# An order written out for the first feed-forward product, with sums begun early and a last product left in PSUM

## The chip, the cores and the metric

The kernel runs on one core of a Trainium2 chip. The core has TensorE (PE) for matmuls, VectorE (DVE), ScalarE (ACT), GpSimd (POOL) and SyncE (SP). Each works through its own list of instructions in order, and semaphores tie the lists together. SP and POOL issue DMA transfers here, and in one place of the changed kernel ACT does. The metric is the time of one execution on the device, in microseconds. The profiled execution is a separate one; its trace is what the times of single instructions are read from.

## The reference

A trunk of two layers over 512 positions of width 1024, in float32. Each layer has an attention part (two kinds of heads) and a feed-forward part; a last norm follows. What matters here is the feed-forward part:

```python
h = rmsnorm(x, mlp_norm[l])
u = jnp.square(jax.nn.relu(jnp.einsum('bsd,df->bsf', h, w_ff1[l])))   # 1024 -> 4096
x = x + jnp.einsum('bsf,fd->bsd', u, w_ff2[l])                        # 4096 -> 1024
...
return rmsnorm(x, final_norm)
```

## The kernel before

**Arithmetic.** A float32 matmul is made of three in a reduced type: each operand is split into a high part and a low rest, and `three` (L281 to L285) adds hi x hi (L283), hi x lo and lo x hi (L284, L285; lines named by the operands in the profile). Every weight tile of 128x1024 must so be split before TensorE uses it: ACT rounds it into `whi` (L125), then DVE takes the difference `wlo` (L126). Weight units are numbered through the kernel. A unit's split is written a few units ahead of its matmuls (`W.next`, `do_split`), into a small ring of pairs of buffers, so that a split waits until an earlier pair is used up.

**The feed-forward part** goes in four groups of the hidden width for each layer, eight in all: L0 g0 to g3, L1 g0 to g3. In a group both products are done by a Strassen-like scheme with seven instead of eight part products:

- The first product has seven "q" products, in the order `HALVES` = 1, 2, 5, 6, 7, 3, 4, each in two halves c = 0, 1 of 24 matmuls of 128x256. Their results add up in PSUM banks: products 1, 6, 7 and 4 share bank a (names f10.. with c), 2 has its own, 5 and 3 share b.
- Between them stand the taps (`tap`): product 1 is copied to F1 by ACT (L907); 2 is added by DVE (L909) and bent, that is relu and square by ACT (L903, L904, `bend`); 6 is copied to F0 (L912); 7 is copied to F2 (L914), has b added (L915) and is bent; 3 is added to F0 (L920) and bent; 4 is bent into F3 straight from PSUM. Since 7 adds onto the same bank as 6, its matmuls wait for the copy of 6.
- The second product has seven forms, `FORMS` = 11, 21, x1, 22, x2, x3, x4, each in two halves of 12 matmuls of 128x512. Their left operand is a table F that is split too (`roll`, L231): Ah and Al, for the x forms Ahx and Alx. DVE adds their results to Y (L948).

**Weights that are sums.** The raw weights of products 7, 5, 6 and 3 are sums of quarters of the weight matrix. Quarters named 11, 12, 21, 22 are loaded by SP (`fill`, L783); a second quarter is added by an accumulating DMA issued by POOL, or a tile is added by DVE (`sum1`, L795):

- tile y: 11 = weight of product 1; later y + 21 = weight of 7 (POOL, L797);
- tile z: 12 = weight of product 2;
- tile x: 21 + 22 = weight of 5 (POOL, L785); then x + y = weight of 6 (DVE); then that + z = weight of 3 (DVE);
- tile w: 22 = weight of 4.

Each tile exists for both halves c (names q00/q01 for x, yw00/yw01 or q10/q11 for y, q20/q21 for z, ww and cs for w). `then(kind, g, form, c, fn, ...)` hangs a function behind the split of that unit. The weights of the forms are fetched by SP (L802) and for the sum forms added by POOL (L809).

**What sets the order.** Within an engine a scheduler places what the program writes, by dependencies and its own estimate. `line(a, v)` overrides it: every operation given to it is chained behind the one given before on ACT or on DVE. Before, the splits of units "f" and "q", the rolls of the forms, the results of forms and some of the tail go through `line`; taps and sums don't.

**The tail.** In the last group `gather` adds x4's results onto Y (L948), `square` sums the squares of a row of tiles (L983), `root` adds the parts (L988) and POOL raises them to -1/2 (L990), `weigh` multiplies by the final gains (L994), and `store` scales and stores (L1000, L1002, DMA on SP).

Of the kernel before, what the change touches and what calls it, by code (L numbers as in the profile page):

```python
# [48 lines left out]
HALVES = ("1", "2", "5", "6", "7", "3", "4")  # L49
FSLOT = {"11": 1, "21": 3, "x1": 4, "22": 3, "x2": 1, "x3": 0, "x4": 2}  # L50
# [112 lines left out]
def trunk(ctx, tc, xT, w, w1, w2, gains, gfin, lamv, cos, sin, out):  # L163
    nc = tc.nc
# [154 lines left out]
    for l in range(L):  # L319
        last = l == L - 1  # L320
        with ExitStack() as actx:
# [470 lines left out]
            def sum1(what, g, c):  # L792
                i = _AT[("q", l, g, "5", c)]
                t, by = W.raw[i], W.raw[_AT[("q", l, g, "1" if what == "y" else "2", c)]]
                nc.vector.tensor_add(t, t, by)  # L795
                if what == "y":
                    nc.gpsimd.dma_start(by, quad1(g, "21", c), accum_op=ALU.add)  # L797
# [50 lines left out]
            for g in range(GROUPS):  # L848
                for c in range(GP // 2):
                    then("q", g, "5", c, sum1, "y", g, c)  # L850
                    then("q", g, "6", c, sum1, "z", g, c)
                    then("q", g, "2" if g else "7", c, fetch, g, "21", c)
                    then("q", g, "7", c, fetch, g, "22", c)
                    then("q", g, "3", c, fetch, g, "11", c)
                    if g:
                        then("q", g, "5", c, fill, "w", g, c)
# [7 lines left out]
                    if g + 1 < GROUPS:  # L864
                        then("q", g, "7", c, fill, "y", g + 1, c)
# [11 lines left out]
        with ExitStack() as fctx:  # L877
# [20 lines left out]
            def tap(q, c, pt):  # L898
# [3 lines left out]
                def bend(n, scale=1.0, src=None):  # L902
                    nc.scalar.activation(f(n), f(n) if src is None else src, AF.Relu, scale=scale)  # L903
                    nc.scalar.activation(f(n), f(n), AF.Square)  # L904

                if q == "1":
                    nc.scalar.copy(f(1), pt)  # L907
                elif q == "2":
                    nc.vector.tensor_add(f(1), f(1), pt)  # L909
                    bend(1)  # L910
                elif q == "6":
                    nc.scalar.copy(f(0), pt)  # L912
                elif q == "7":
                    nc.scalar.copy(f(2), pt)  # L914
                    nc.vector.tensor_add(f(2), f(2), sums[("b", c)])  # L915
                    bend(2, -1.0)
                elif q == "4":
                    bend(3, -1.0, pt)
                elif q == "3":
                    nc.vector.tensor_add(f(0), f(0), pt)  # L920
                    bend(0)
# [10 lines left out]
            def less(o, i, j):  # L932
                nc.vector.scalar_tensor_tensor(
                    out=F[o], in0=F[i], scalar=-1.0, in1=F[j], op0=ALU.mult, op1=ALU.subtract)
# [28 lines left out]
            def lay(tb, j):  # L963
                o = place(tb, j)
                n = 24 * j + tb
                nc.vector.scalar_tensor_tensor(
                    out=o, in0=turned(tb, j), scalar=fin[:, n : n + 1], in1=o, op0=ALU.mult, op1=ALU.add)
# [228 lines left out]
```

## Time and profile before

| | us |
|---|---|
| median of three runs | 1145.57 |
| lowest and highest run | 1143.81, 1146.23 |
| the profiled execution's own time | 1145.74 |
| its span in the profile | 1144.0 |
| TensorE busy | 1118.7 |
| VectorE, ScalarE, GpSimd busy | 923.9, 707.9, 173.5 |
| DMA moved | 183.39 MB |

The span is what the engines and queues of the core cover in the trace; 1.74 us of the execution lie around it. A row of the trace in order of time has start and duration in us, the engine, the line, the operation, output <- input, and in brackets the idle time of that engine ahead of it with what ended it. A row of the waits has who waited <- for whom: us in total, times, longest. A group's matmuls on product 7 appear as `f<-T_hi,whi`, since all the products share L283.

### The profile page before, as it was taken

What the parts mean: (1) busy time and instruction counts of PE and PEld (TensorE: products, weight loads), DVE (VectorE), ACT (ScalarE), POOL (GpSimd) and SP (SyncE); (2) the same over time, 40 slices, a digit from 0 to 9 for tenths busy, and PEclk for the clock granted to TensorE, in tenths of its full rate; (3) what the DMA queues carried; (4) which work ended last, traced back from release to release, by engine and by line L of the source; (5) the groups of instructions that cost most, each with busy time, mean ns of one, the idle gap of its engine ahead of it and who ended that gap; (6) DMA issues with size and microseconds to landing.
All of it is one profiled execution on the core that took longest, in us unless ns stands there. A gap on an engine that the chain in (4) does not pass through costs nothing. (4 is left out here: it accounts for less than half of the span.)

```text
span 1144.0 us, 18030 instructions
## 1 busy us (share of the span) xinstructions
PE 1118.7 (98%) x6834; PEld 996.7 (87%) x6834; DVE 923.9 (81%) x1238; ACT 707.9 (62%) x1121; POOL 173.5 (15%) x253
## 2 busy tenths in 40 slices
PE   9999999999998999999999999999999999999996
PEld 7889889899898898899878898888998998988985
DVE  6898778898886877877879876887978788788786
ACT  6456666677747547557545566665777575565674
POOL 1001432110110110201000024231101102011012
PEclk9999999999999999999999999999999999999998
DMA  7664443255886776886526844423568858859764
GB/s 254 178 177 138 127 132 111 101 133 170 189 200 179 153 189 181 186 212 171 113 74 184 204 115 125 147 93 127 114 198 173 219 148 187 219 119 206 209 133 125
DMA packets 60470, 183.39 MB, mean 160 GB/s; under 512 B 7520, under 2 KB 8544, under 8 KB 60384
## 3 DMA queue, kind: packets, MB, share of 16 engines
q1 hardware_dynamic: 46416, 131.88, 35.9%
q0 software_dynamic: 13824, 50.34, 25.1%
q8 instruction: 54, 0.88, 0.3%
q14 instruction: 32, 0.26, 0.1%
q10 hardware_dynamic: 144, 0.02, 0.0%
HBM read 154.95 MB, written 2.10 MB: 137 GB/s over the span
## 5 line engine op out<-in xcount | busy, mean ns | idle before, releaser
L126 DVE TENSOR_TENSOR wlo<-q,whi 128x1024 fp32r<-128x1024 f32 x184 | 223.1, 1220 | 29.4 <-ACT whi L125 28.9
L125 ACT ACTIVATE whi<-q 128x1024 fp32r<-128x1024 f32 x184 | 189.2, 1050 | 68.6 <-DMA q<-in_w 31.6
L283 PE MATMUL f<-T_hi,whi 128*128 128x256 f32 x512 | 146.6, 286 | 7.7 <-ACT F L912 7.6
L284 PE MATMUL f<-T_lo,whi 128*128 128x256 f32 x512 | 145.6, 284 | 0.0
L285 PE MATMUL f<-T_hi,wlo 128*128 128x256 f32 x512 | 145.5, 284 | 0.0
L809 POOL DMA_DIRECT2D q<-in_w x64 | 56.2, 912 | 367.9 <-DVE wlo L126 348.2
L283 PE MATMUL f<-h_hi,whi 128*128 128x256 f32 x384 | 109.8, 286 | 1.0 <-DVE F L915 0.9
L284 PE MATMUL f<-h_lo,whi 128*128 128x256 f32 x384 | 108.6, 283 | 0.0
L285 PE MATMUL f<-h_hi,wlo 128*128 128x256 f32 x384 | 108.6, 283 | 0.0
L283 PEld LDWEIGHTS f<-T_hi,whi 128*128 128x128 f32 x512 | 98.9, 193 | 9.2 <-ACT F L912 9.2
L285 PEld LDWEIGHTS f<-T_hi,wlo 128*128 128x128 f32 x512 | 99.0, 193 | 0.0
L284 PEld LDWEIGHTS f<-T_lo,whi 128*128 128x128 f32 x512 | 98.9, 193 | 0.0
L126 DVE TENSOR_TENSOR wlo<-raw,whi 128x1024 fp32r<-128x1024 f32 (+1 forms) x68 | 79.2, 1172 | 7.6 <-ACT whi L125 7.5
L125 ACT ACTIVATE whi<-raw 128x1024 fp32r<-128x1024 f32 (+1 forms) x68 | 66.3, 982 | 29.4 <-PE p1d1q L284 6.4
L283 PEld LDWEIGHTS f<-h_hi,whi 128*128 128x128 f32 x384 | 73.5, 192 | 2.5 <-DVE F L915 1.6
L284 PEld LDWEIGHTS f<-h_lo,whi 128*128 128x128 f32 x384 | 73.6, 192 | 0.3
L285 PEld LDWEIGHTS f<-h_hi,wlo 128*128 128x128 f32 x384 | 73.6, 192 | 0.1
L231 ACT ACTIVATE Ahx<-F 128x1024 fp32r<-128x1024 f32 x32 | 33.9, 1061 | 53.6 <-PE x L284 23.7
L231 DVE TENSOR_TENSOR Alx<-F,Ahx 128x1024 fp32r<-128x1024 f32 x32 | 39.2, 1226 | 9.4 <-ACT Ahx L231 9.4
L126 DVE TENSOR_TENSOR wlo<-yw,whi 128x1024 fp32r<-128x1024 f32 x24 | 29.3, 1222 | 15.5 <-ACT whi L125 15.5
L125 ACT ACTIVATE whi<-yw 128x1024 fp32r<-128x1024 f32 x24 | 25.3, 1054 | 26.3 <-DMA yw<-in_w 24.7
L904 ACT ACTIVATE F<-F 128x512 f32<-128x512 f32 x64 | 40.2, 630 | 1.5
(950 smaller groups left out, 3316.7 us busy)
## 6 DMA issues: line engine op xcount, KB each, us to landing
q<-in_w SPq DMA_DIRECT2D x100, 512.0 KB, 4.7
q<-in_w POOLq DMA_DIRECT2D x84, 512.0 KB, 6.4
raw<-in_w SPq DMA_DIRECT2D x62, 512.0 KB, 4.0
yw<-in_w SPq DMA_DIRECT2D x12, 512.0 KB, 4.8
yw<-in_w POOLq DMA_DIRECT2D x12, 512.0 KB, 7.9
cs<-in_w SPq DMA_DIRECT2D x8, 512.0 KB, 4.6
ww<-in_w SPq DMA_DIRECT2D x8, 512.0 KB, 4.7
x<-in_xT SPq DMA_DIRECT2D x8, 256.0 KB, 4.5
```

Of the source, the lines that this page charges most:

```text
L125: h = nc.scalar.activation(hi[:, a:b], raw[:, a:b], AF.Copy)
L126: self.last = h, nc.vector.tensor_tensor(out=lo[:, a:b], in0=raw[:, a:b], in1=hi[:, a:b].bitcast(F32), op=ALU.subtract)
L231: return nc.scalar.activation(hi, src, AF.Copy), nc.vector.tensor_tensor(out=lo, in0=src, in1=hi.bitcast(F32), op=ALU.subtract)
L283: nc.tensor.matmul(pt, ah, bh, start=first, stop=False, skip_group_check=onto)
L284: nc.tensor.matmul(pt, ah, bl, start=False, stop=False, skip_group_check=onto)
L285: nc.tensor.matmul(pt, al, bh, start=False, stop=last, skip_group_check=onto)
L809: paced(nc.gpsimd.dma_start(t, quad(g, q, c), accum_op=ALU.add))
L904: nc.scalar.activation(f(n), f(n), AF.Square)
```

## The change

The names of the functions stay, the line numbers shift (in the changed kernel whi is L126, wlo L127, product 1's copy L912, product 2's add L914, bends L908 and L909, product 6's copy L917, product 7's copy and add L919 and L920, product 3's add L925, the rolls L232, results of forms L953).

1. The accumulation of 21 onto y is issued behind the split of product 1 (`grow_y`). The weight of 6 is then the new y plus w (`sum_y`), behind 5's second split for c = 0 and behind 6's first for c = 1; the weight of 3 is that plus z (`sum_z`). The load of w moves to the form stage of the group before, and that of form 21's weights from product 2 to 5.
2. All taps, bends, sums, rolls and differences of the feed-forward part go through `line`, so ACT and DVE keep the order in which the program writes them: the split that is due, then the product's tap.
3. In the last group x4's PSUM banks take x3's sum with Y added in place, squares and stores read PSUM, part of the adding for the norm moves to POOL, and the very last store is issued by ACT.
4. The places at which x is laid into Y in layer 1's middle groups are given by a table `LAYS`.

```diff
+LAYS = (("5", 1), ("6", 0), ("6", 1), ("7", 0))
...
-            def sum1(what, g, c):
-                i = _AT[("q", l, g, "5", c)]
-                t, by = W.raw[i], W.raw[_AT[("q", l, g, "1" if what == "y" else "2", c)]]
-                nc.vector.tensor_add(t, t, by)
-                if what == "y":
-                    nc.gpsimd.dma_start(by, quad1(g, "21", c), accum_op=ALU.add)
+            def grow_y(g, c):
+                nc.gpsimd.dma_start(W.raw[_AT[("q", l, g, "7", c)]], quad1(g, "21", c), accum_op=ALU.add)
+
+            def sum_y(g, c):
+                t, by, w = (W.raw[_AT[("q", l, g, q, c)]] for q in "674")
+                line(v=nc.vector.tensor_add(t, by, w))
+
+            def sum_z(g, c):
+                t, by = (W.raw[_AT[("q", l, g, q, c)]] for q in "32")
+                line(v=nc.vector.tensor_add(t, t, by))
...
-                    then("q", g, "5", c, sum1, "y", g, c)
-                    then("q", g, "6", c, sum1, "z", g, c)
-                    then("q", g, "2" if g else "7", c, fetch, g, "21", c)
+                    then("q", g, "1", c, grow_y, g, c)
+                    then("q", g, "56"[c], 1 - c, sum_y, g, c)
+                    then("q", g, "6", c, sum_z, g, c)
+                    then("q", g, "5" if g else "7", c, fetch, g, "21", c)
...
-                    if g:
-                        then("q", g, "5", c, fill, "w", g, c)
...
                     if g + 1 < GROUPS:
+                        then("f", g, "11", c, fill, "w", g + 1, c)
...
                 def bend(n, scale=1.0, src=None):
-                    nc.scalar.activation(f(n), f(n) if src is None else src, AF.Relu, scale=scale)
-                    nc.scalar.activation(f(n), f(n), AF.Square)
+                    line(nc.scalar.activation(f(n), f(n) if src is None else src, AF.Relu, scale=scale))
+                    line(nc.scalar.activation(f(n), f(n), AF.Square))
...
                 elif q == "6":
-                    nc.scalar.copy(f(0), pt)
+                    line(nc.scalar.copy(f(0), pt))
...
+            def finish_row(tb, pt):
+                if tb == 0:
+                    store(2, 0)
+                    store(2, 1)
+                square(tb, 0, pt)
+                root(tb, 0)
+                if tb == 0:
+                    store(3, 0)
+                    store(3, 1)
+                    store(0, 0, pt)
+                else:
+                    store(0, 1)
+                    store(1, 0, pt)
+                    store(1, 1, None, nc.scalar)
...
+                        elif tail and form == "x3":
+                            line(v=nc.vector.tensor_add(to[r], to[r], place(r, 0)))
...
```

How this moves instructions, in the group L0 g2 (whi92 to whi101 are the splits of 5 c0, 5 c1, 6 c0, 6 c1, 7 c0, 7 c1, 3 c0, 3 c1, 4 c0, 4 c1; F10 is product 2's table, F00 that of 6 and 3, F20 that of 7).

ACT, from the split of 5 c1 to the first copy of product 6, before:

```order
L125 ACTIVATE whi93_4409<-q01_0_2671 128x1024
L907 COPY F10_2679<-f1020_4383 128x512
L907 COPY F10_2679<-f1021_4416 128x512
L125 ACTIVATE whi94_4442<-q00_0_2670 128x1024
L125 ACTIVATE whi95_4475<-q01_0_2671 128x1024
L903 ACTIVATE F10_2679<-F10_2679 128x512
L904 ACTIVATE F10_2679<-F10_2679 128x512
L125 ACTIVATE whi96_4512<-yw00_2870 128x1024
L903 ACTIVATE F10_2679<-F10_2679 128x512
L904 ACTIVATE F10_2679<-F10_2679 128x512
L231 ACTIVATE Ah110_4508<-F10_2679 128x1024
```

and in the changed kernel:

```order
L126 ACTIVATE whi93_4409<-q01_0_2671 128x1024
L912 COPY F10_2679<-f1021_4415 128x512
L126 ACTIVATE whi94_4441<-q00_0_2670 128x1024
L908 ACTIVATE F10_2679<-F10_2679 128x512
L909 ACTIVATE F10_2679<-F10_2679 128x512
L126 ACTIVATE whi95_4475<-q01_0_2671 128x1024
L908 ACTIVATE F10_2679<-F10_2679 128x512
L909 ACTIVATE F10_2679<-F10_2679 128x512
L232 ACTIVATE Ah110_4508<-F10_2679 128x1024
L126 ACTIVATE whi96_4512<-yw00_2872 128x1024
```

The bends of product 2 have moved ahead of the splits whi95 and whi96; three splits and then the copy of product 6 follow in both.

DVE over the same stretch, before:

```order
L126 TENSOR_TENSOR wlo93_4410<-q01_0_2671,whi93_4409 128x1024
L795 TENSOR_TENSOR q00_0_2670<-q00_0_2670,yw00_2870 128x1024
L795 TENSOR_TENSOR q01_0_2671<-q01_0_2671,yw01_2871 128x1024
L126 TENSOR_TENSOR wlo94_4443<-q00_0_2670,whi94_4442 128x1024
L909 TENSOR_TENSOR F10_2679<-F10_2679,f2020_4447 128x512
L795 TENSOR_TENSOR q00_0_2670<-q00_0_2670,q20_0_2674 128x1024
L126 TENSOR_TENSOR wlo95_4476<-q01_0_2671,whi95_4475 128x1024
```

and in the changed kernel:

```order
L127 TENSOR_TENSOR wlo93_4410<-q01_0_2671,whi93_4409 128x1024
L798 TENSOR_TENSOR q00_0_2670<-yw00_2872,ww0_2874 128x1024
L127 TENSOR_TENSOR wlo94_4442<-q00_0_2670,whi94_4441 128x1024
L802 TENSOR_TENSOR q00_0_2670<-q00_0_2670,q20_0_2674 128x1024
L798 TENSOR_TENSOR q01_0_2671<-yw01_2873,cs_76 128x1024
L914 TENSOR_TENSOR F10_2679<-F10_2679,f2020_4447 128x512
L127 TENSOR_TENSOR wlo95_4476<-q01_0_2671,whi95_4475 128x1024
```

Two sums now stand between wlo94 and the add of product 2, and the second y sum has moved behind wlo94.

POOL, around weight 5 of the group, before:

```order
L809 DMA q01_0_2671<-in_w2 128x1024
L785 DMA q00_0_2670<-in_w1 128x1024
L785 DMA q01_0_2671<-in_w1 128x1024
L797 DMA yw00_2870<-in_w1 128x1024
L797 DMA yw01_2871<-in_w1 128x1024
```

and in the changed kernel:

```order
L814 DMA q01_0_2671<-in_w2 128x1024
L786 DMA q00_0_2670<-in_w1 128x1024
L794 DMA yw00_2872<-in_w1 128x1024
L786 DMA q01_0_2671<-in_w1 128x1024
L794 DMA yw01_2873<-in_w1 128x1024
```

The first accumulation onto y has moved between the two of weight 5. Further on, ACT has the bends of 7 between the splits of 4 and of form 11; from the split of 4 c0 on, in the changed kernel (before, whi101 and whi102 stood ahead of the first bend):

```order
L126 ACTIVATE whi100_4634<-ww0_2874 128x1024
L919 COPY F20_2680<-f1020_4383 128x512
L908 ACTIVATE F20_2680<-F20_2680 128x512
L909 ACTIVATE F20_2680<-F20_2680 128x512
L126 ACTIVATE whi101_4666<-cs_76 128x1024
L919 COPY F20_2680<-f1021_4415 128x512
L908 ACTIVATE F20_2680<-F20_2680 128x512
L909 ACTIVATE F20_2680<-F20_2680 128x512
L126 ACTIVATE whi102_4698<-q00_0_2670 128x1024
```

Each split now stands behind the bends of the half before it. TensorE at the start of form 21, in the changed kernel (before, each pair of Ah matmuls was followed by its Al, and the matmul of x1 stood in its own form):

```order
L286 MATMUL 11021_4835<-whi103_4731,Al110_4509 128x512
L284 MATMUL 21020_4862<-whi104_4767,Ah210_4829 128x512
L285 MATMUL 21020_4862<-wlo104_4768,Ah210_4829 128x512
L284 MATMUL 21021_4863<-whi104_4767,Ah210_4829 128x512
L285 MATMUL 21021_4863<-wlo104_4768,Ah210_4829 128x512
L284 MATMUL x1020_4906<-whi106_4880,Ahx10_4876 128x512
L286 MATMUL 21020_4862<-whi104_4767,Al210_4830 128x512
```

The first matmul with Al210 has moved behind one of x1, which needs the table Ahx10 and the split whi106.

More of the change, by code (lines that the diff above doesn't have):

```diff
@@ L919, in tap @@
                 elif q == "3":
[L920 removed]
+                    line(v=nc.vector.tensor_add(f(0), f(0), pt))
                     bend(0)
@@ L1051, in trunk @@
                                 less(3, 1, 3)
-                            if last and g in (1, 2) and q in "5673":
-                                lay("5673".index(q), g - 1)
                 chains = {}
@@ L1073, in trunk @@
                         W.do_split(W.used + 1 + r, first)
[L1074 to L1084 removed]
+                        tail = end and last
                         if end and not last and form in ("21", "x2", "x3", "x4"):
                             line(v=add_to(tb, j, to[r]))
+                        elif tail and form == "x4":
+                            finish_row(r, to[r])
                         else:
```

74 lines of the change are left out of this document (34 added, 40 removed).

## Prediction

> **What bounds the kernel now.** I read the busy times first, then the chain of waits by engine, then the places that it names in order of time. Line numbers are those of the kernel before. First, TensorE's busy line and waits:
>
> ```profile
> PE 1118.7 (98%) x6834; PEld 996.7 (87%) x6834; DVE 923.9 (81%) x1238; ACT 707.9 (62%) x1121; POOL 173.5 (15%) x253
> PE f L283 <- ACT F L912: 7.6, 6, 3.1
> PE f L283 <- DVE F L915: 0.9, 2, 0.5
> ACT whi L125 <- DMA yw<-in_w: 24.7, 8, 5.2
> ```
>
> TensorE has little left to give. What the change can win in the feed-forward part is 7.6 + 0.9 us: product 7 waits for the copy that empties its PSUM bank of product 6 (L912), and product 3 for L915. What it can lose is larger, since TensorE is the bound nearly everywhere: any list of ACT and DVE that ends after its product is due comes out at the end. So I follow one group, layer 0's third, on both engines from the moment when weight 5's second half is there. ACT, then DVE:
>
> ```profile
> 413.31 1.06 ACT L125 ACTIVATE whi<-q 128x1024 fp32r<-128x1024 f32 x1 [2.06 <-DMA q<-in_w]
> 419.81 0.64 ACT L903 ACTIVATE F<-F 128x512 f32<-128x512 f32 x1 [0.73 <-DVE F L909]
> 420.47 0.63 ACT L904 ACTIVATE F<-F 128x512 f32<-128x512 f32 x1
> 424.78 1.06 ACT L125 ACTIVATE whi<-yw 128x1024 fp32r<-128x1024 f32 x1 [3.67 <-DMA yw<-in_w]
> 428.97 1.99 ACT L125 ACTIVATE whi<-q 128x1024 fp32r<-128x1024 f32 x2
> 430.86 0.56 ACT L912 COPY F<-f 128x512 f32<-128x512 f32 x1
> 414.40 1.22 DVE L126 TENSOR_TENSOR wlo<-q,whi 128x1024 fp32r<-128x1024 f32 x1 [1.90 <-ACT whi L125]
> 415.55 2.35 DVE L795 TENSOR_TENSOR q<-q,yw 128x1024 f32<-128x1024 f32 x2
> 417.95 1.23 DVE L126 TENSOR_TENSOR wlo<-q,whi 128x1024 fp32r<-128x1024 f32 x1
> 419.09 0.68 DVE L909 TENSOR_TENSOR F<-F,f 128x512 f32<-128x512 f32 x1
> ```
>
> The start of the list is the landing of weight 5 (413.31), and its end is L912 at 430.86. In between ACT stands idle 3.67 us for weight 7, which the late accumulating transfer brings. These rows give the steps for the sums below: whi to its wlo 1.09; a DVE operation over 1024 columns to the next 1.14 (two take 2.35); L909 0.68; relu to square 0.65 and square to the next 0.53; whi after whi 0.96 (two take 1.99); L912 0.56.
>
> **First part: the list from weight 5 to product 7.** The new order on ACT is: 5's last split, 6 first half, the two bends of product 2 first half, 6 second half, its bends, Ah of form 11, the two splits of 7, 3's first, then the copy of product 6. DVE has two sums for each half between the splits and the adds. From the start S of the split of 5's second half: its wlo 1.09, first y sum to 3.45, whi of 6 at 3.55, wlo at 4.64, z sum 5.78, the second half's y sum 6.92, L909 8.06 to 8.74, relu 8.77, square 9.42, whi of 6's second half only then, 9.95, wlo 11.04, z sum 12.18, L909 13.32, bends 14.03 and 14.68, Ah 15.35, whi 16.31, 17.27 and 18.23, copy L912 19.19 to 19.75, product 7 at S + 19.80. Weight 7 is there early now, so the 3.67 us are gone, but nothing of them is left: the extra z and y sums and the bends ahead of 6's second half have taken their place. The six groups with this order, S first and then product 7's first matmul as it was:
>
> ```profile
> 330.33 1.06 ACT L125 ACTIVATE whi<-q 128x1024 fp32r<-128x1024 f32 x1 [1.38 <-DVE fin L1032]
> 493.82 1.06 ACT L125 ACTIVATE whi<-q 128x1024 fp32r<-128x1024 f32 x1 [0.82 <-DMA q<-in_w]
> 899.86 1.06 ACT L125 ACTIVATE whi<-q 128x1024 fp32r<-128x1024 f32 x1 [2.12 <-DMA q<-in_w]
> 979.13 1.06 ACT L125 ACTIVATE whi<-q 128x1024 fp32r<-128x1024 f32 x1 [2.11 <-DMA q<-in_w]
> 1060.05 1.06 ACT L125 ACTIVATE whi<-q 128x1024 fp32r<-128x1024 f32 x1 [1.41 <-DMA q<-in_w]
> 349.84 0.39 PE L283 MATMUL f<-T_hi,whi 128*128 128x256 f32 x1 [3.10 <-ACT F L912]
> 431.48 0.39 PE L283 MATMUL f<-T_hi,whi 128*128 128x256 f32 x1 [1.34 <-ACT F L912]
> 511.94 0.39 PE L283 MATMUL f<-T_hi,whi 128*128 128x256 f32 x1 [1.47 <-ACT F L912]
> 917.11 0.38 PE L283 MATMUL f<-T_hi,whi 128*128 128x256 f32 x1 [0.99 <-ACT F L912]
> 997.66 0.38 PE L283 MATMUL f<-T_hi,whi 128*128 128x256 f32 x1 [0.15 <-ACT F L912]
> 1077.99 0.38 PE L283 MATMUL f<-T_hi,whi 128*128 128x256 f32 x1
> ```
>
> S + 19.80 less the start before: 0.29, 1.63, 1.68, 2.55, 1.27, 1.86, together **+9.3 us** with weight 5 landing where it does now.
>
> **Where weight 5 lands.** On POOL the early accumulation of y's first half now stands between the two halves of 5 in the same queue.
>
> ```profile
> 403.54 0.88 POOL L785 DMA_DIRECT2D q<-in_w  x1 [11.89 <-DMA q<-in_w]
> 406.11 0.88 POOL L785 DMA_DIRECT2D q<-in_w  x1 [1.70 <-DMA q<-in_w]
> 341.59 1.06 ACT L125 ACTIVATE whi<-yw 128x1024 fp32r<-128x1024 f32 x1 [5.20 <-DMA yw<-in_w]
> 344.09 1.06 ACT L125 ACTIVATE whi<-yw 128x1024 fp32r<-128x1024 f32 x1 [0.25 <-DMA yw<-in_w]
> ```
>
> Its issue alone costs nothing: 0.88 us fit into the 1.70 us that POOL waits for the plain load of the second half. Its bytes don't: two accumulations issued back to back were taken up 2.50 us apart (341.59 and 344.09, both waiting for the transfer), so 5's second half comes 0 to 3 us later. Against that, the loads of w and form 21 leave this stretch. I take half, 1.4 us, six times: **+8.4 us** (bounds 0 and 18). The Trainium skill, page "DMA: Bandwidth & Descriptors", section "Anatomy of one DMA — SWDGE (gpsimd) path", puts the part of a transfer that grows with its size at bytes / 436e9 s, an estimate of 1.2 us for 512 KB. By that the term would be 7.2 us; the trace's 2.50 us say that sharing makes it more.
>
> **The two first groups of the layers** have opening operations in the same lists. There weight 5 is early, and the pace is DVE's:
>
> ```profile
> 817.10 1.22 DVE L826 TENSOR_TENSOR hx1mdl<-hx1mdl 128x1024 f32<-128x1024 f32 x1
> 834.35 0.28 PE L283 MATMUL f<-T_hi,whi 128*128 128x256 f32 x1
> 266.12 0.39 PE L283 MATMUL f<-T_hi,whi 128*128 128x256 f32 x1 [0.56 <-ACT F L912]
> ```
>
> In layer 1, 5's second wlo now takes the place at 817.10. Nine DVE steps follow up to L909 (wlo, L828, y sum, two T_lo, wlo, L834, z sum, y sum, 9 x 1.14): 827.36. Then bends to 829.25, whi and wlo to 831.4, z sum, L909 to 833.2, bends, Ah, three splits as above, copy to 839.0: product 7 at 839.05 against 834.35, +4.7. The same list in layer 0 gives 270.7 against 266.12, +4.6. Together **+9.3 us** (bounds 0 and 12).
>
> **The clock.** Product 7 was due at its start less its wait (431.48 - 1.34 in the group shown). Against that, the lists of the six groups end 1.4 to 3.5 us late, and with the 1.4 us of the queue 2.8 to 4.9; the first groups' gaps are of 4.7 to 5.2 us. The granted clock behind the gap of 3.10 us and behind that of 1.34:
>
> ```profile
> 349.90:354.40 4.50, 4.50 (x26) 4.50 (x27) 2.19 (x2) 1.60 (x3) 0.00 (x0) 0.64 0.91 344
> 431.50:436.00 4.50, 4.50 (x37) 4.50 (x38) 2.80 (x4) 2.83 (x4) 0.00 (x0) 1.00 0.94 339
> ```
>
> PEclk is the column behind POOL. After 3.1 us idle it was 0.64 for 4.5 us, 1.6 us lost; after 1.34 us idle it was 1.00. One group pays already. Of the other seven, whose gaps lie around the 3.10 us that paid, I let four pay: **+6.5 us** (0 to 11.3). The Trainium skill, page "TensorE: Matmul & The Clock Gate", section "What's actually happening", halves the clock after at least one idle window of about 3.4 us, free-running. If every gap holds a whole window all seven pay and the sum is 4.8 us higher. The trace agrees as far as its two cases go, with the break between 1.34 and 3.10 us.
>
> **Second part: products 7, 3, 4 and form 21.** Now each half's copy, add and two bends must be done before ACT takes the next split, and the next add waits for that split's wlo. A half costs 1.09 + 1.14 + 0.68 + 0.03 + 1.19 = 4.13 us on this zigzag, where TensorE needs 24 x 0.12 = 2.88 us. Before, splits ran ahead of bends:
>
> ```profile
> 450.66 1.06 ACT L231 ACTIVATE Ah<-F 128x1024 fp32r<-128x1024 f32 x1
> 451.76 1.23 DVE L231 TENSOR_TENSOR Al<-F,Ah 128x1024 fp32r<-128x1024 f32 x1 [1.02 <-ACT Ah L231]
> 454.63 0.39 PE L283 MATMUL 21020_4860<-whi,Ah 128*128 128x512 f32 x1
> ```
>
> Al is there 1.64 us before form 21 starts. From the start of product 7's second half, the new list gives: L914 0.2, L915 0.8, splits at 2.70, 6.83, 10.96 and 15.09, last split 17.2, bends of product 4 to 19.4, Ah 19.43, Al 20.52 to 21.75, Ahx 20.39, first split of x1 21.35 to 22.41. Form 21 is due at 5 x 2.88 + 2 x 2.73 = 19.87. TensorE has four matmuls that need Ah alone, and in six groups then one of x1, before the first with Al; at 0.227 us each that one is due at 21.01 and starts at 22.79: 1.78 late; in the two first groups, without x1's, 1.1. Six times 1.78 and twice 1.1 are **+12.9 us**. The bound below is 0, if the bends overlap better than this; above, 18. L915 no longer holds product 3: **-0.9 us**. No other queue hides it: SP's loads and POOL's sums of the second matrices are all issued earlier than their splits.
>
> **Third part: the tail.** The last PSUM bank isn't added to Y any more, and the last store has a queue of its own.
>
> ```profile
> 1136.51 0.68 DVE L948 TENSOR_TENSOR Y<-Y,11131_11340 128x512 f32<-128x512 f32 x1
> 1137.29 0.63 ACT L983 ACTIVATE F<-Y 128x512 f32<-128x512 f32 x1 [0.72 <-DVE Y L948]
> 1138.97 0.75 DVE L1002 SCALAR_TENSOR_TENSOR Y<-Y,fin,cs 128x512 f32<-128x512 f32 x1 [0.66 <-POOL fin L990]
> ```
>
> The square can start when ACT has done two stores and the other row's square, about 1134.8 instead of 1137.29: **-2.4 us** (-1 to -3.5). The two added sums onto PSUM (as L909, 0.68 us) lie a form ahead of x4 on DVE, beside its matmuls.
>
> **At nothing** I put these. SP's loads of w stand a whole form stage earlier (they are first read at weight 5, a group's first products later). The load of form 21's weights moves from product 2 to 5, on the same queue, still six products ahead of its use. The transposes and adds that lay x into Y in layer 1's middle groups (0.68 us of DVE each, as L909) move a product or so within the stretch in which TensorE now waits anyway; without that gap they would cost TensorE what they cost it before. POOL's two added sums for the last norm stand beside the last form. Behind ACT's new wait for L909 the splits of 6, 7 and 3 are queued, and DVE's wlo of each: that is the list counted above, not a second price.
>
> **Sum.** 9.3 + 8.4 + 9.3 + 6.5 + 12.9 - 0.9 - 2.4 = +43.1 us. The profiled execution took 1145.74 us (span 1144.0; the median of the runs is 1145.57), so 1188.8; forecast **1188**.
>
> **Rivals.** (a) Weight 5 lands as before and the clock holds in the new gaps: 8.4 and 6.5 fall away, 1174. For it speaks that the loads of w and 21 leave; against it the 2.50 us. (b) Every gap pays and the queue costs 3 us: 1188.8 + 9.6 + 4.8 = 1203. (c) Faster: weight 5's second half lands early, as loads have left the stretch. It decides where S lies 19.80 us before product 7 is due, 1.4 to 3.5 us earlier than now. Then 7.6, 0.9, the 1.6 of the clock and 2.4 go, and form 21 costs at best 8 x 1.1: 1145.7 - 12.5 + 8.8 = 1142. Against it: an accumulation was put ahead in its queue. (d) As (c), form 21 at its full price: 1146, no change.
>
> **How the numbers follow.** The forecast has 0.52, with a range of its own of 1178 to 1198; (a) 0.22; (b) 0.10; (c) 0.10; (d) 0.06. From (a)'s lower side to (b), 1163 to 1204 hold 0.82. A change of 0.2% (2.3 us) is what can be told from none: faster 0.10, same 0.06, slower 0.84.
>
> **What would show it.** Waits of product 7 on 6's copy of 2.8 us or more in all eight groups; the idle time of whi ahead of weight 7 gone; a wait of form 21 on Al or of x on its split; PEclk under 1.0 behind the gaps; the last store sooner behind the last matmul. I am wrong if TensorE goes from product 6 to 7 without a gap, or if Al of form 21 is still early.

## The result and the profile after

| | before | changed |
|---|---|---|
| median of the runs, us | 1145.9 | 1214.19 |
| lowest and highest run | 1143.81, 1147.61 | 1211.19, 1216.39 |
| ratio, 95% interval | | 1.0595 (1.0566 to 1.0624) |
| the profiled execution (span) | 1145.74 (1144.0) | 1211.19 (1209.4) |

The change makes the kernel slower by 68 us. The sign was forecast, and the size was not: 1188 was expected and the range ended at 1204. First the busy line of the changed kernel's page:

```profile
PE 1139.8 (94%) x6834; PEld 1007.5 (83%) x6834; DVE 921.8 (76%) x1238; ACT 709.3 (59%) x1121; POOL 175.8 (15%) x257
```

Its waits by engine (us in total, times, longest; L917 is now product 6's copy, L126 the split, L914 the add of product 2 and L908 its bend):

```profile
PE f L284 <- ACT F L917: 37.5, 8, 4.7
PE f L286 <- DVE wlo L127: 4.7, 6, 0.9
PE f L284 <- ACT whi L126: 3.0, 5, 1.0
PE x L284 <- ACT whi L126: 4.0, 6, 0.7
ACT whi L126 <- DMA q<-in_w: 73.1, 34, 5.4
ACT F L908 <- DVE F L914: 58.1, 16, 5.2
```

TensorE's share falls from 98% to 94%, and its wait on product 6's copy grows from 7.6 to 37.5 us. It now comes once in each of the eight groups. Ahead of that wait, product 6's second half now waits for its own split in six groups, 4.7 us in all for the rest and 2.0 of the 3.0 us for the high part, where it didn't wait before. ACT waits 73.1 us for raw weights where it waited 31.6 and 24.7 before, and the bends of product 2 wait 58.1 us for DVE's add, where they waited 4.3. TensorE's busy time also grew, by 21 us, with the same matmuls. In the order of time, POOL, ACT and then TensorE's first matmul of product 7, in the same group as before (L0 g2, whose first matmul starts at 421.86):

```profile
418.53 0.88 POOL L786 DMA_DIRECT2D q<-in_w  x1 [11.59 <-DMA q<-in_w]
419.96 0.88 POOL L794 DMA_DIRECT2D yw<-in_w  x1 [0.55 <-DVE wlo L127]
421.85 0.89 POOL L786 DMA_DIRECT2D q<-in_w  x1 [1.02 <-DMA q<-in_w]
426.12 1.06 ACT L126 ACTIVATE whi<-q 128x1024 fp32r<-128x1024 f32 x1 [4.36 <-DMA q<-in_w]
431.04 1.06 ACT L126 ACTIVATE whi<-q 128x1024 fp32r<-128x1024 f32 x1 [3.39 <-DMA q<-in_w]
434.59 1.06 ACT L126 ACTIVATE whi<-q 128x1024 fp32r<-128x1024 f32 x1 [2.01 <-DVE q L798]
439.93 0.63 ACT L908 ACTIVATE F<-F 128x512 f32<-128x512 f32 x1 [4.29 <-DVE F L914]
441.13 1.04 ACT L126 ACTIVATE whi<-q 128x1024 fp32r<-128x1024 f32 x1
445.32 0.63 ACT L908 ACTIVATE F<-F 128x512 f32<-128x512 f32 x1 [3.15 <-DVE F L914]
446.65 1.06 ACT L232 ACTIVATE Ah<-F 128x1024 fp32r<-128x1024 f32 x1
447.61 1.99 ACT L126 ACTIVATE whi<-yw 128x1024 fp32r<-128x1024 f32 x2
450.45 0.56 ACT L917 COPY F<-f 128x512 f32<-128x512 f32 x1
451.06 0.58 PE L284 MATMUL f<-T_hi,whi 128*128 128x256 f32 x1 [4.69 <-ACT F L917]
```

The same stretch of time as windows, the gap and what stands behind it, then cut where the clock changes (second column TensorE's busy time and its matmuls, behind POOL the granted clock, then the DMA share and GB/s):

```profile
442.24:451.06 8.82, 3.38 (x24) 2.97 (x24) 6.34 (x6) 5.67 (x8) 0.00 (x0) 0.85 0.00 1
451.06:455.56 4.50, 4.50 (x22) 4.50 (x23) 3.60 (x4) 2.34 (x3) 0.00 (x0) 0.53 0.94 301
448.50:455.30 6.80, 4.24 (x20) 4.24 (x21) 6.16 (x6) 4.90 (x7) 0.00 (x0) 0.50 0.58 183
455.40:458.00 2.60, 2.60 (x24) 2.60 (x23) 0.69 (x1) 1.16 (x2) 0.00 (x0) 1.00 1.04 414
```

S, the start of the split of weight 5's second half, is 431.04, 4.92 us behind the split of the first half: the early accumulation onto y (419.96) was issued between the two. From there the list is the one that the prediction wrote down: 6's second half is split at S + 10.09 (counted: 9.95), Ah at S + 15.61 (15.35), the copy at S + 19.41 (19.19), product 7 at S + 20.02 (19.80). The wait for weight 7 (3.67 us before) is gone, and no time came of it. In the 4.5 us behind the gap the clock is 0.53, where the same place had 1.00 before: it was 0.50 from the middle of the gap to 455.30, and 1.00 from there. So 22 matmuls fit in instead of 37; 13.8 of TensorE's 21 us of added busy time are of this kind (product 7's halves in the eight groups).

Form 21 in the same group on TensorE, then the tail (the last matmul, ACT's last square, DVE's last store), in the order of time:

```profile
476.47 0.50 PE L284 MATMUL 21020_4862<-whi,Ah 128*128 128x512 f32 x1 [0.53 <-ACT Ah L232]
478.36 0.50 PE L284 MATMUL x<-whi,Ahx 128*128 128x512 f32 x1 [0.70 <-ACT whi L126]
478.70 0.39 PE L286 MATMUL 21020_4862<-whi,Al 128*128 128x512 f32 x1
1201.18 0.39 PE L286 MATMUL 11131_11340<-whi,Alx 128*128 128x512 f32 x1
1203.04 0.57 ACT L988 ACTIVATE F<-11131_11340 128x512 f32<-128x512 f32 x1
1204.56 0.75 DVE L1008 SCALAR_TENSOR_TENSOR Y<-11131_11340,fin,cs 128x512 f32<-128x512 f32 x1 [0.66 <-POOL fin L996]
```

Form 21 waits for its table, and then one matmul of x1 for its split, as counted. In the tail the last square starts 1.9 us behind the last matmul, where it was 3.9 behind it before.

Product 7's first matmul against the group's first, and S, in all the groups (us; worked out from the starts of the matmuls and of the split in the two traces; in g1 of both layers other work lies between the first two matmuls and the rest, so there the start is the second half's less 2.88 us):

| group | S before | S changed | product 7 before | changed | S to product 7 changed |
|---|---|---|---|---|---|
| L0 g0 | 4.0 | 5.0 | 23.8 | 29.4 | 24.4 |
| L0 g1 | 6.9 | 7.8 | 26.4 | 27.9 | 20.1 |
| L0 g2 | 6.4 | 9.2 | 24.5 | 29.2 | 20.0 |
| L0 g3 | 6.5 | 9.7 | 24.7 | 29.8 | 20.0 |
| L1 g0 | 3.8 | 5.8 | 23.0 | 30.0 | 24.2 |
| L1 g1 | 7.9 | 9.0 | 25.1 | 29.1 | 20.1 |
| L1 g2 | 5.7 | 9.3 | 24.2 | 29.4 | 20.0 |
| L1 g3 | 5.4 | 9.5 | 23.3 | 29.5 | 20.0 |

Summed over the eight groups, the span's 65.4 us lie here: from the first matmul to product 7 +39.3; product 7 itself (both halves, the slow clock) +13.8; products 3 and 4 -3.1; forms 11 and 21 +13.9; the last forms x3 and x4 +3.4; the tail -2.4 (10.6 to 8.2 us from the start of the last matmul to the end of the span); the rest lies between the stages.

### The profile page after: what moved, and what is told of

Same layout as the page of the kernel before. It is cut to its first block, busy times and chain, and to the rows that moved or that the text cites. A ratio compares the mean times of both kernels' runs of the same rounds, so it can differ in the third digit from the quotient of the medians.

```text
span 1209.4 us, 18024 instructions
## 1 busy us (share of the span) xinstructions
PE 1139.8 (94%) x6834; PEld 1007.5 (83%) x6834; DVE 921.8 (76%) x1238; ACT 709.3 (59%) x1121; POOL 175.8 (15%) x257
## 3 DMA queue, kind: packets, MB, share of 16 engines
q0 software_dynamic: 13824, 50.34, 23.3%
## 4 chain that ended last, share of the span: by engine, by line
PE 41%; DVE 20%; DMA 13%; ACT 12%; issue 11%; POOL 1%; SPq 0%; POOLq 0%; DVEq 0%; ACTq 0%
DMA q<-in_w 12%; DVE wlo L127 8%; ACT whi L126 6%; ACT F L908 2%; ACT F L909 2%; DVE q L798 1%; PE f L284 1%; PE wo L284 1%; PE wo L286 1%; PE wo L285 1%; PE f L285 1%; PE f L286 1%; PE x L284 1%; DVE Al L232 1%; PE x L286 1%
## 5 line engine op out<-in xcount | busy, mean ns | idle before, releaser
L127 DVE TENSOR_TENSOR wlo<-q,whi 128x1024 fp32r<-128x1024 f32 x184 | 222.5, 1221 | 109.1 <-ACT whi L126 108.9
L126 ACT ACTIVATE whi<-q 128x1024 fp32r<-128x1024 f32 x184 | 190.8, 1050 | 94.8 <-DMA q<-in_w 73.1
L284 PE MATMUL f<-T_hi,whi 128*128 128x256 f32 x512 | 153.5, 300 | 39.6 <-ACT F L917 37.5
L286 PE MATMUL f<-T_hi,wlo 128*128 128x256 f32 x512 | 151.6, 296 | 4.8 <-DVE wlo L127 4.7
L285 PE MATMUL f<-T_lo,whi 128*128 128x256 f32 x512 | 151.0, 295 | 0.0
L284 PEld LDWEIGHTS f<-T_hi,whi 128*128 128x128 f32 x512 | 104.8, 205 | 42.4 <-ACT F L917 39.1
L286 PEld LDWEIGHTS f<-T_hi,wlo 128*128 128x128 f32 x512 | 104.6, 204 | 6.2 <-DVE wlo L127 6.2
L285 PEld LDWEIGHTS f<-T_lo,whi 128*128 128x128 f32 x512 | 104.9, 205 | 0.0
L908 ACT ACTIVATE F<-F 128x512 f32<-128x512 f32 x48 | 30.4, 632 | 103.9 <-DVE F L914 58.1
L127 DVE TENSOR_TENSOR wlo<-raw,whi 128x1024 fp32r<-128x1024 f32 (+1 forms) x68 | 79.2, 1172 | 7.7 <-ACT whi L126 7.6
L126 ACT ACTIVATE whi<-raw 128x1024 fp32r<-128x1024 f32 (+1 forms) x68 | 66.2, 982 | 29.7 <-PE p1d1q L285 6.4
L232 ACT ACTIVATE Ahx<-F 128x1024 fp32r<-128x1024 f32 x32 | 33.8, 1058 | 22.4 <-PE x L285 17.3
L232 DVE TENSOR_TENSOR Al<-F,Ah 128x1024 fp32r<-128x1024 f32 x24 | 29.3, 1221 | 19.6 <-ACT Ah L232 19.6
L232 DVE TENSOR_TENSOR Alx<-F,Ahx 128x1024 fp32r<-128x1024 f32 x32 | 39.1, 1220 | 4.7 <-ACT Ahx L232 4.6
L232 ACT ACTIVATE Ah<-F 128x1024 fp32r<-128x1024 f32 x24 | 25.4, 1060 | 28.1 <-DVE Y L953 4.0
```

Source lines behind the costliest of these rows:

```text
L126: h = nc.scalar.activation(hi[:, a:b], raw[:, a:b], AF.Copy)
L127: self.last = h, nc.vector.tensor_tensor(out=lo[:, a:b], in0=raw[:, a:b], in1=hi[:, a:b].bitcast(F32), op=ALU.subtract)
L232: return nc.scalar.activation(hi, src, AF.Copy), nc.vector.tensor_tensor(out=lo, in0=src, in1=hi.bitcast(F32), op=ALU.subtract)
L284: nc.tensor.matmul(pt, ah, bh, start=first, stop=False, skip_group_check=onto)
L285: nc.tensor.matmul(pt, ah, bl, start=False, stop=False, skip_group_check=onto)
L286: nc.tensor.matmul(pt, al, bh, start=False, stop=last, skip_group_check=onto)
```

## Experiments

Three theories share the loss. L, the lists: the fixed order makes the time from S to product 7 long, and form 21's table late. Q, the queue: the early accumulation holds up weight 5, so S is late. C, the clock: each long gap is paid twice. The rival to L as the main cause is Q with C. The edits are given against the changed kernel unless said otherwise. The kernel before ran beside each of three sets of runs, and the ratios are to those: its median was 1148.41 us beside the runs of the queue alone, no chain, the chain alone and 24 unread matmuls, 1146.32 beside the one without bends and sums in the chain and the one with y first, and 1145.83 beside the others. The times of S below are counted from the group's first matmul, as in the table.

**The queue alone.**

```diff
-                    nc.gpsimd.dma_start(t, quad1(g, "22", c), accum_op=ALU.add)
+                    fives[c] = nc.gpsimd.dma_start(t, quad1(g, "22", c), accum_op=ALU.add)
...
-                nc.gpsimd.dma_start(W.raw[_AT[("q", l, g, "7", c)]], quad1(g, "21", c), accum_op=ALU.add)
+                behind(nc.gpsimd.dma_start(W.raw[_AT[("q", l, g, "7", c)]], quad1(g, "21", c), accum_op=ALU.add), fives[1])
```

> The changed kernel with one edit: on POOL the two accumulations of weight 5 come first in every group, the two early accumulations onto y behind them. Three theories share the 68 us. Q (the queue): the early accumulation holds up weight 5's second half, so the split S of that half begins later against the group's first matmul than before the change (7.7 to 9.7 us, before 5.3 to 7.8). L (the lists): from S to product 7 the fixed order takes 20.1 us whatever the queue does. C (the clock): each gap over some 3 us ahead of product 7 costs 1.7 us or more again. If Q holds as counted, S comes back by about 2.7 us in the six later groups, 16 us, the chain stays at 20.1 to 20.3, and some gaps fall under what the clock punishes: 1187 to 1199 us. If weight 5 was late for another reason (the load of its first quarter, or all transfers slowed), S stays and the time is within 3 us of 1214.

1197.88 us, 1193.64 to 1201.76; ratio to before 1.0418 (1.0376 to 1.046). As Q has it: S is at 5.9 to 7.9 us in the six later groups, and S to product 7 stays at 20.2 to 20.3 us in each (ACT and TensorE in L0 g2, then TensorE's wait on product 6's copy, here L919):

```profile
429.41 1.06 ACT L126 ACTIVATE whi<-q 128x1024 fp32r<-128x1024 f32 x1 [2.08 <-DMA q<-in_w]
449.71 0.58 PE L284 MATMUL f<-T_hi,whi 128*128 128x256 f32 x1 [4.68 <-ACT F L919]
PE f L284 <- ACT F L919: 32.9, 8, 4.7
```

So Q is worth 16 us by the medians and 20 by the ratios (1.0595 less 1.0418), and L holds whatever S is. S didn't come back all the way: it had moved by 15.9 us in the sum of the six groups, 12.0 of them went with this edit, and 3.9 stayed.

**No chain.**

```diff
-                    line(nc.scalar.activation(f(n), f(n) if src is None else src, AF.Relu, scale=scale))
-                    line(nc.scalar.activation(f(n), f(n), AF.Square))
+                    nc.scalar.activation(f(n), f(n) if src is None else src, AF.Relu, scale=scale)
+                    nc.scalar.activation(f(n), f(n), AF.Square)
... (and so for the copies, adds, sums, roll 11, differences, and the adds that lay x into Y)
```

> The changed kernel with only its second part undone: copies, adds, bends, sums, the roll of form 11 and the differences are no longer chained, so the scheduler places them; the early accumulation, the new sums and the tail stay. L (the lists make nearly all of it): from S to product 7 about 15 us instead of 20.1, the gaps ahead of product 7 about 1.5 us instead of 6, so the clock stays full, and form 21 has its table in time again: 1214 - 29 - 10 - 14 - 14 = about 1147, between 1140 and 1156. Q (the queue makes half of it): S stays late by 2.7 us and the gaps stay at 3 us or more with the clock low, 1165 to 1180.

1143.33 us, ratio to before 0.9967 (0.994 to 0.9993). The 68 us are gone, and perhaps a little more. Its trace is that of the longest of its ten runs (1151.08 us), so it shows the order of things and not the last 5 us. Its waits at TensorE:

```profile
PE f L284 <- ACT F L917: 10.0, 6, 2.2
PE f L284 <- DVE F L920: 1.8, 3, 1.2
```

S and product 7 of L0 g2, in the order of time:

```profile
418.95 1.06 ACT L126 ACTIVATE whi<-q 128x1024 fp32r<-128x1024 f32 x1 [3.98 <-DMA q<-in_w]
434.06 0.39 PE L284 MATMUL f<-T_hi,whi 128*128 128x256 f32 x1 [2.18 <-ACT F L917]
```

S is as late as in the changed kernel (8.3 to 10.3 us in the six later groups), yet product 7 comes 15.1 us behind it, as expected. So the late weight costs next to nothing by itself (product 7 and 3 wait 11.8 us in all, in the kernel before 8.5): Q's 16 us are paid only because the fixed list behind S leaves no slack. Without L, neither Q nor C costs more than a few us here.

**The chain alone**, put into the kernel before (same edit as above, the other way round, with that kernel's own sums).

> The kernel before with only the second part of the change: copies, adds, bends, sums, the roll of form 11 and the differences chained in program order; its own sums and its late accumulation onto y stay, and its tail. By L counted from the rows of before, S to product 7 is then about 17.5 us (one sum less stands ahead of the second half's bends than in the changed kernel), so with S where it is before, product 7 waits 0 to 2.5 us, less than before, and nearly the whole price is form 21's, 13 to 14 us: 1150 to 1160. If the fixed order alone is the cause of the 68 us (L without Q), gaps of 5 us stand ahead of product 7 here too: 1190 to 1214.

1178.79 us, ratio 1.0255 (1.0223 to 1.0288): missed, between the two expectations. S to product 7 was 17.7 to 17.8 us in five later groups (18.2 in the sixth), counted 17.5. Two things had been left out: the first groups, where the list alone made gaps of 5.8 and 4.8 us, and S, which lay at 7.0 to 9.3 us without any edit of the queue, 6.6 us later in the sum of the six groups than in the kernel before. So the chain itself delays S too. TensorE's wait on product 6's copy:

```profile
PE f L283 <- ACT F L912: 21.0, 8, 4.7
```

So of the 68 us the chain makes 30 on its own; the rest needs the chain and the early sums and transfers together.

**Unread matmuls in the gaps.**

```diff
+                        if q == "6" and c:
+                            pf = bank("t", f"fill{l}{g}")
+                            for k in range(24):
+                                op = nc.tensor.matmul(pf, h_hi[:, 0, 0:128], h_hi[:, 0, :], start=True, stop=True)
... (chained behind product 6's last matmul, and product 7's first behind them)
```

> The changed kernel with 24 matmuls of 128x512 whose result nobody reads, put on TensorE between products 6 and 7 in every group (24 x 0.227 = 5.4 us, where the gaps are 4.8 to 6.1 us). C (the clock): the work behind the gap runs at full clock, products 7's halves take 2.88 us each again instead of 4.4 to 5.3 for the first, and the 13.8 us lost there go: 1199 to 1203. If the matmuls behind the gap are slow for another reason (late weights, busy transfers), they stay slow and the time stays within 3 us of 1214.

1219.25 us (1216.64 to 1222.14): missed. The clock did what C says, since product 7's halves took 2.88 us in the six groups without transposes. But in layer 1's two middle groups the first unread matmul waited for a PSUM bank, which DVE's addition of x frees late in the fixed order, and these gaps grew to 12.5 and 15.1 us. Again with 20, and none in those groups:

> As the run with 24 unread matmuls, but with 20 of them, and none in layer 1's two middle groups: there the earlier run's matmuls had to wait for a PSUM bank that a DVE addition frees, 15.8 us that have nothing to do with the question. C (the clock): six gaps stay as they are in the changed kernel (20 x 0.227 = 4.5 us are covered by 4.8 us and more) and product 7's halves behind them run at full clock: 12.2 us of the 16.9 lost there in all eight groups go, 1200 to 1204.

1206.01 us (1201.13 to 1210.77), 8 us less than the changed kernel by the medians and 2 above the range expected. The same place as above, TensorE's row of them and then two windows:

```profile
444.54 4.72 PE L1055 MATMUL fill<-h_hi 128*128 128x512 f32 x20
445.00:449.50 4.50, 4.37 (x20) 3.31 (x19) 3.44 (x4) 4.50 (x6) 0.00 (x0) 1.00 0.02 5
449.50:454.00 4.50, 4.50 (x38) 4.50 (x39) 4.17 (x5) 2.90 (x5) 0.00 (x0) 1.00 0.91 340
```

Product 7 still starts when it did (29.6 us behind the first matmul, 29.2 in the changed kernel), the clock behind the gap is 1.00 instead of 0.53, and 38 matmuls fit in at a DMA share of 0.91. So the slow matmuls come from the gap, not from busy transfers. In the six groups 11.7 of the 12.2 us lost on product 7 came back; 3.5 us of it went to later starts of product 7 in the eight groups and 4.4 to form 21 in the first ones. Why these came was not tried.

**Which part of the chain.** First the bends alone taken out:

> The changed kernel with only the bends (relu and square) taken out of the chain; copies, adds, sums, roll and differences stay chained. The scheduler then puts the splits of 6's second half and of 4, 11 one place ahead of the bends. Of the two lists: from S to product 7 it gives 18.7 us instead of 20.1, since DVE's two sums per half stay where they are; in products 7, 3, 4 a split no longer waits for the bends of the half before, so the table of form 21 is there in time and its 14 us go. Together 1214 - 14 - 11 = 1189, between 1183 and 1195. If the bends' place were all of it, the time would be that of the run without the chain, 1141 to 1151; if the adds' and sums' place were all of it, 1210.

1182.74 us, ratio 1.0329 (1.0303 to 1.0355). A little under what was expected: S to product 7 is 18.3 to 18.4 us in five of the six later groups (20.0 in the sixth; counted 18.7), and form 21 on time in all six of them (late by 1.3 and 2.0 in the first groups). Its wait at product 7 is still there:

```profile
PE f L284 <- ACT F L917: 29.0, 7, 4.9
```

Then the two sums of raw weights too, with copies, adds, roll and differences still chained:

> The changed kernel with the bends and the two sums of raw weights taken out of the chain; copies, adds, roll and differences stay chained. With the bends alone taken out it was 1183, with all of it 1143. By the list that the scheduler then makes, the first half's y sum stands ahead of S and one sum less between 6's split and the adds: S to product 7 about 14 us instead of 18.4, so with S at 9.2 us product 7 waits under 1 us in the six later groups: 1140 to 1150, as the run without any chain. If the copies' and adds' place carries the rest, it stays near 1183.

1150.15 us, ratio 1.0031 (1.0016 to 1.0046), at the upper end of the expectation. S to product 7 is 14.7 to 17.2 us, and the wait at product 7 is a third of what it was:

```profile
PE f L284 <- ACT F L917: 10.4, 6, 2.7
```

Taken out in this order, the bends' place is worth 31 us, the sums' 33, and the other operations' some 7, of which 4 in the first groups, where form 21 is still 2 us late.

**Better orders of the queue.** Without the chain and with weight 5 first:

> The two edits of the earlier runs together: the changed kernel with nothing of products chained, and with weight 5's two accumulations ahead of the early ones onto y. In the run without the chain S lies 8.2 to 10.2 us behind the first matmul of the six later groups and product 7 still waits 0.4 to 2.3 us; the run with the queue put right brought S back by 2 to 3.5 us. If both add, S to product 7 stays at 14.5 to 16 us, S is at 6 to 8 us, and product 7 is due first (S + 16 is before 23.04 us), so its waits of 11 us in all eight groups go: 1132 to 1138, faster than both kernels. If the scheduler's list ends late for another reason than S, the waits stay and the time is that of the run without the chain, 1141 to 1146.

1144.08 us, ratio 0.9987 (0.9965 to 1.001): the gain missed, the time that of the run without the chain. S came back to 5.2 to 8.4 us, but the second y sum then waits for its transfer, and S to product 7 is 16.8 to 18.4 us. Its row in L0 g2 (DVE):

```profile
416.95 1.23 DVE L800 TENSOR_TENSOR q<-yw,cs 128x1024 f32<-128x1024 f32 x1 [2.59 <-DMA yw<-in_w]
```

And with both accumulations onto y first:

> The changed kernel with nothing of products chained (as in the run without the chain) and, on POOL, both early accumulations onto y ahead of weight 5's. The run with them behind weight 5 missed its forecast: S came back to 5 to 8 us, but from S to product 7 it took 18 us instead of 15, since the second y sum then had to wait for its transfer. If the queue moves one accumulation each 2.5 us whatever stands first, four of them end 9 us behind the first matmul: S stays at 9 us here, but the first half's y sum no longer waits for S, the list from S shrinks to some 12.5 us, and product 7 is due first: its 10 us of waits go, 1132 to 1138. If POOL's wait for the split of product 1's second half pushes weight 5 further back, S lies at 10 us or more and the waits stay: 1142 to 1148.

1153.23 us, ratio 1.0061 (1.0046 to 1.0076): the mechanism of the second case named there, but 5 us above its range. POOL's accumulation has to wait for the split that still reads y, everything behind it with it, and S lies at 10.6 to 12.8 us (POOL):

```profile
407.78 0.87 POOL L796 DMA_DIRECT2D yw<-in_w  x1 [1.85 <-DVE wlo L127]
408.32 1.25 POOL L786 DMA_DIRECT2D q<-in_w  x1
```

S to product 7 shrank to 12.8 us in four groups (13.9 in the two others), yet in all three orders of the queue tried without the chain product 7 came 23 to 26 us behind the first matmul. The wait moved along the queue and didn't go.

**The tail alone**, put into the kernel before:

> The kernel before with only the third part of the change: the last product's banks take Y, squares and stores read PSUM, two store queues. By the trace of the changed kernel the end of the span stands some 2 us nearer to the last matmul. Expected 2 to 3 us less than the kernel before, ratio 0.9975 to 0.9985; no effect on anything ahead of the last form. If the gain of the tail was not real, 1.000.

1143.63 us, ratio 0.9988 (0.9971 to 1.0006): the size expected, but the runs can't tell it from no change. The trace can: from the start of the last matmul to the end of the span 7.7 us, before 10.6.

The run without the chain is the only version whose interval (0.994 to 0.9993) lies wholly under the kernel before, a gain of 0.3%; beside the one with the tail alone it is the same within what was measured, so most of its gain may be the tail's.

## Why the prediction was right or wrong

The mechanism was the forecast one: the list of ACT and DVE ends after product 7 is due, at every group, and the gap is paid again with the clock. The sum was 22.3 us short (43.1 counted, 65.4 measured in the spans). Where weight 5 lands and the clock make 7.4 and 7.3 of it, the first groups 3.3, forms x3 and x4 3.4, the list 1.5, form 21 1.0; products 3 and 4 gave 2.2 back.

- **The list from S to product 7: right.** 19.80 us counted, 20.02 to 20.10 measured in six groups of six.
- **Where weight 5 lands: the first of the two terms that failed.** The term took "half, 1.4 us". S moved 0.9 to 4.1 us, 15.9 in total instead of 8.4, near the upper bound of 18. The two halves' landings are 5.0 us apart in five groups of the changed kernel (7.0 in the sixth), two steps of 2.50; before they were 2.5 to 3.7 apart. "The loads of w and form 21 leave this stretch" was given as much weight as a measured spacing, with no row behind it. Not all of it is the queue: 12.0 us went with weight 5 put first, and the chain alone made S later by 6.6 us, for which the prediction's sum has no term. That sharing makes the 2.50 us, as the prediction has it, no run shows; and the two accumulations that it was read from were issued 3.76 us apart, not back to back, though they landed 2.5 us apart.
- **The first groups: short by 3.3 us**, 2.3 of it in layer 1. The prediction said "there weight 5 is early", but on POOL the early accumulations stand ahead of it there too, and both halves landed 4 to 5 us later. In L1 g0 the split of the first half then waits 3.1 us for its transfer, and S is 2.0 us later. With weight 5 put first S is back at 3.8 us, and product 7 is late by 4.9 us, where 4.7 had been counted; with the queue as changed, by 7.0. In L0 g0 S is 1.0 us later and no split waits for a transfer; S lies between 4.0 and 5.1 us there in all the traces (4.7 with the tail alone), and what sets it is open.
- **The clock: the second term, half of it missed.** Four of seven new gaps were let pay 1.6 us. All of them paid, and the eight together cost 13.8 us more than before instead of 6.5. By the prediction's own sums, with the queue's 1.4 us, six of the seven new gaps were longer than the 3.10 us that had paid, so that choosing four had no ground; all seven at 1.6 us would have been 11.3. The rest is the size of the price, 1.4 to 2.7 us: the granted clock was 0.50 for 6.83 us in five of the groups and for 3.41 in three, and what of that lies behind the gap is paid.
- **Form 21: right.** 12.9 counted, 13.9 measured; forms 11 and 21 took 1.8 us longer in five of the six later groups (counted 1.78; 1.4 in the sixth), 1.7 and 1.8 in the first ones (1.1). Without the chained bends that was gone in the six later groups.
- **Product 3's wait: gone**, as said. Products 3 and 4 together gained 3.1 us, not 0.9: some 0.9 are transposes of x that `LAYS` moves from product 3 to product 7 in layer 1's two middle groups, and the rest is spread over all the groups in pieces of 0.1 to 0.3 us.
- **The tail: right**, -2.4 counted and -2.4 measured in the changed kernel.
- **What was not counted:** +3.4 us in forms x3 and x4, whose splits wait for weights. It was 1.6 to 1.8 in three of the runs (the queue, the chain alone, no chain), 0.7 without bends and sums in the chain, 0.1 or less in three others (bends out, and both better orders of the queue), and over 3 in the two with unread matmuls; what makes it is open.
- **The rivals.** (b), every gap paying and the queue costing 3 us, came nearest with 1203. The measured values add the first groups, the last forms and the size of the clock's price to it. (c) and (d) needed weight 5 earlier than before, and its second half came later in all eight groups.

Why a fixed order costs so much is shown by the three runs that open it step by step: 1214, 1183 without the bends, 1150 without the sums too, 1143 without any.

## What to carry to other kernels

Before two in-order engines are given an order by hand, write the list from the last thing that arrives from outside (here a transfer) to the first thing that is due, with the spacings of the trace. If its length exceeds the time between them, every microsecond of a later arrival comes out at the end. An order that lets work for later stages stand behind what is due cost next to nothing here for the same late arrival. Where a sum needs several transfers of one queue, count the landing of the last; in the orders tried here, moving them only moved the wait.

A gap on the engine that bounds the kernel should be priced with the clock behind it. If the known case of that price is shorter than the gaps forecast, count all of them as paying, as all 24 gaps of 2.72 us and more did here.

## What the runs showed of the hardware

In ten of the traces (all but the two with unread matmuls), six groups each, without layer 1's middle ones (their transposes blur the measure), the idle time ahead of product 7 (from the start of product 6's second half to product 7, less the 2.88 us of that half; rows of the trace give up to 0.3 us less for the same gap) against the time that product 7's two halves took over 5.76 us. The nine cases under 0.95 us are left out:

| idle ahead of product 7, us | cases | of them with the slow clock | price, us |
|---|---|---|---|
| 0.95 to 1.92 | 18 | 0 | 0.1 |
| over 1.92 to 2.34 | 9 | 5 | 1.5 to 1.6, else 0.1 to 0.4 |
| 2.72 to 6.14 | 24 | 24 | 1.3 to 2.7 |

Near 2 us it's the place of the gap that decides. In each trace the granted clock changes only at times that lie whole multiples of 3.41 us apart (the end of the kernel excepted), and behind a gap that pays it's 0.50 for one or two such stretches. Cut at these times, each of the 35 gaps of the ten traces that paid, all eight groups taken, left TensorE idle for 1.76 us or more within one stretch, and each of the 45 that didn't for 1.74 us or less. Two gaps of the run with the chain alone, each in two neighbouring stretches (second column TensorE's busy time, behind POOL the granted clock):

```profile
353.84:357.25 3.41, 2.54 (x22) 2.34 (x20) 2.14 (x2) 3.38 (x5) 0.00 (x0) 1.00 0.00 0
357.25:360.66 3.41, 2.22 (x18) 2.22 (x19) 3.41 (x4) 3.41 (x5) 0.00 (x0) 1.00 0.63 184
1108.19:1111.60 3.41, 1.65 (x14) 1.44 (x13) 3.41 (x4) 3.41 (x5) 0.00 (x0) 1.00 0.19 64
1111.60:1115.01 3.41, 3.41 (x19) 3.41 (x18) 2.39 (x3) 1.18 (x3) 0.00 (x0) 0.50 0.96 358
```

The first gap, 2.06 us, is cut in two (0.87 and 1.19 us idle) and didn't pay; the second, 1.76 us, lies in one stretch and paid 1.6 us. By this count a gap under 1.74 us doesn't lower the clock, one of 3.5 us always does, since half of it lies in one stretch however it's cut, and between them it depends on where it falls. The two cases of the kernel before (1.34 and 3.10) left that open.

The Trainium skill, page "TensorE: Matmul & The Clock Gate", section "What's actually happening", has the clock halved after at least one idle window of about 3.4 us. The price and the length of the window fit, but a window a little over half idle already paid here, and the 3.10 us of the kernel before, which the prediction took for agreement, were shorter than a whole one. Where the two differ, the measurement decides.

The accumulating transfers of 512 KB from POOL's queue landed in the order of their issue in all twelve traces, most often 2.5 us apart where one waited behind another. In the changed kernel's L0 g2 weight 5's first half, the early y and weight 5's second half landed at 426.0, 428.5 and 431.0 us.
